# The last two squares of a planned norm: added on VectorE in place of summed as parts on TensorE

## The chip, the cores and the metric

The kernel runs on one core of one Trainium2 chip. The metric is device time in microseconds, the median of several executions. Engines are called by the profile's names: PE (TensorE, matrix products), DVE (VectorE), ACT (ScalarE), POOL (GpSimd), SP (the queue that issues most loads). Each engine runs its instructions in the order in which they were put; they wait for each other by semaphores.

## The reference

A two-layer decoder trunk on one sequence of 512 tokens with a model width of 1024, in float32. Each layer is half a SwiGLU block, a mixer, and half a SwiGLU block; each of the six begins with an RMS norm. Cut to what matters:

```python
def rms_norm(x, g):
    xf = x.astype(jnp.float32)
    y = xf * lax.rsqrt(jnp.mean(xf * xf, axis=-1, keepdims=True) + EPS) * g.astype(jnp.float32)
    return y.astype(x.dtype)

for l in range(DEPTH):
    x = x + 0.5 * swiglu(rms_norm(x, ffn_norm[l, 0]), ...)
    h = rms_norm(x, mix_norm[l])
    x = x + m          # m: hybrid_mixer(h, ...) in layer 0, sparse_attention(h, ...) in layer 1
    x = x + 0.5 * swiglu(rms_norm(x, ffn_norm[l, 1]), ...)
```

What concerns the change is the mean of `xf * xf` over the 1024 features of each token.

## The kernel before

The residual stream lies in SBUF as `xT`, features on partitions: eight blocks `xT[:, j]` of 128 features x 512 tokens. Six stages run one after the other: ffn00, mix0 (the hybrid mixer), ffn01, ffn10, mix1 (attention), ffn11. Every product is made three times from operands split into a high and a low part (`mm3`, L280 to L282): high x high, high x low, low x high. Weights are loaded in blocks (tile `raw`, on SP), split by ACT (L500 or L239) and DVE (L502 or L242) into `form` (or `iw`, `wq` in attention), and multiplied. In some blocks ("summed") the low part is made by a DMA that POOL issues (L529 to L531).

The norm of the next stage is prepared at the end of each stage. The normalising factor of a token is not applied to the input of the next products; they take x times the gain (`xgn`, high and low, L795 on ACT and L798 on DVE), and the factor follows on their results. So the products of the next stage can begin before the factor is known.

`prep_later(which, k, last, ...)` puts this preparation of the blocks k and k+1 into a plan. For each block j: `xgn`, then a square on ACT (L809) into one of four buffers. Block 0's square goes to the buffer `ssq` itself. For the others but the last two, POOL adds the square to `ssq` (`vtt` with `pool=True`, recorded at L495). The last two blocks (j = 4 and 5 behind an FFN, 6 and 7 behind attention) aren't added: their squares are put into the list `ssqs` beside `ssq`, with the first token block for which they count.

`settle_later` then puts, at two fixed places within the first unit of the next stage, the rest: `sums` on PE (L416), one matmul of 128x128 by a column of ones for each of the four token blocks and each part in `ssqs`, into the PSUM tile `pssq`; a scale on DVE (L762); a power on POOL (L764); later transposes on PE into `prow` (L437) and a copy on ACT (L768) into `rrow`, which the evacuation of the first products and the forms of x (L582) read. Behind ffn00, where the mixer's part isn't planned, `settle` and `rms_col` do the same (L428, L429, L464).

What sets the order: `Plan` collects steps with an engine, an estimated duration, reads and writes, computes due times back from PE's stream, and places the steps one by one. PE's steps of one stream stay in the order in which they were added; the steps of the other engines are chosen by when they can start, then by due time. Steps of `vtt` on POOL are estimated at 0.1 us + 2.5 ns per element of a row, on DVE at 0.15 us + 1.05 ns, and the sums at 0.2 us + 0.45 us per part. The mixer of layer 0 is ordered by the scheduler of the language instead. So a changed step can move others of the plan.

Planned norms are four: for mix0, ffn10, mix1 and ffn11. The first norm has no squares of this kind (`load_x`), and the norm for ffn01 is made by `prep`, without a plan; neither is touched. In the norm for ffn11 the squares of blocks 0 to 3 are made and added by halves of 256 tokens.

Of the kernel before, what the change touches and what calls it, by code (L numbers as in the profile page):

```python
# [13 lines left out]
ALU = mybir.AluOpType  # L14
# [4 lines left out]
NB = T // P  # L19
# [194 lines left out]
class Trunk:  # L214
# [557 lines left out]
    def prep_later(self, which, k, last, squares=True, half=None):  # L772

        nc = self.nc
        if k == 0 and not half:
            self.which = which
            self.xgn = [[Lazy(lambda: self.part.tile([P, 4, T], F32R, name="xgn", tag="xg")) for _ in range(2)] for _ in range(2)]  # L780
            squares4 = Lazy(lambda: self.tmp.tile([P, 4, T], F32, name="ssq", tag="ssq", bufs=1))
            self.sqs = [lambda i=i: squares4()[:, i] for i in range(4)]
            self.ssq = self.sqs[0]
            self.ssqs, self.ssqk = [(self.ssq, 0)], ["ssq"]
            self.xg = [LazyFeat(t) for t in self.xgn]
            self.xgk = lambda k: [("xg", which, i, k) for i in range(2)]
        xgn, xT, ssq = self.xgn, self.xT, self.ssq
        halves = (0, 1) if half is None else (half,)
        cols = slice(halves[0] * H, halves[-1] * H + H)
        n = cols.stop - cols.start  # L790
        for j in (k, k + 1):
            g, x = self.gain(which, j), xT[:, j, cols]
            hi, lo = (lambda i=i, j=j: xgn[i][j // 4]()[:, j % 4, cols] for i in range(2))
            hik, lok = ([("xg", which, i, j)] for i in range(2))
            self.s(n, lambda hi=hi, x=x, g=g: nc.scalar.activation(hi(), x, AF.Copy, scale=g), self.xk(j, halves), hik)  # L795

            def low(hi=hi, lo=lo, x=x, g=g, j=j):
                ins = nc.vector.scalar_tensor_tensor(lo(), x, g, hi().bitcast(F32), op0=ALU.mult, op1=ALU.subtract)  # L798
                if j == 0:
                    self.mark = ins  # L800

            self.v(n, low, self.xk(j, halves) + hik, lok)
            if not squares:
                continue
            if j == 0:
                sq, sk = ssq, ["ssq"]
            else:
                sq, sk = self.sqs[1 + j % 3], [("sq", j % 3)]
            self.s(n, lambda x=x, sq=sq: nc.scalar.activation(sq()[:, cols], x, AF.Square), self.xk(j, halves), sk)  # L809
            if last:  # L810
                self.ssqs, self.ssqk = self.ssqs + [(sq, halves[0] * NB // 2)], self.ssqk + sk
            elif j:
                part = [lambda x=x: x()[:, cols] for x in (ssq, sq)]
                self.vtt(n, part[0], *part, ALU.add, ["ssq"], ["ssq"] + sk, True)
        if last:
            self.pending = 1 + squares

# [1076 lines left out]
```

## Time and profile before

| | |
|---|---|
| median of 3 runs | 2018.12 us (2016.62 to 2026.48) |
| profiled execution, its own time | 2019.29 us |
| its span | 2017.6 us |
| mean granted PE clock | 0.992 |
| ACT busy | 1170.2 us |
| instructions | 34412 |

The span is the time from the first to the last recorded instruction. The profile comes as a page (busy times, slices, chain of waits, costliest groups) and as views of the trace. A row of the timeline gives the start, the length in us, the engine, the line of the kernel, the operation, the tile written and the tiles read, shapes and a count; in brackets stands how long the engine was idle before it and what ended that idle time. Rows of the waits and of single tiles give minimum, median and maximum in ns. Rows of the stretches give the length, the busy time of PE, PE's weight loads, DVE, ACT and POOL with counts, the granted PE clock (1.00 is full), the share of the DMA engines, and GB/s. Matmul lengths overlap, so their pace is read from starts.

### The profile page before, as it was taken

What the parts mean: (1) busy time and instruction counts of PE and PEld (TensorE: products, weight loads), DVE (VectorE), ACT (ScalarE), POOL (GpSimd) and SP (SyncE); (2) the same over time, 40 slices, a digit from 0 to 9 for tenths busy, and PEclk for the clock granted to TensorE, in tenths of its full rate; (3) what the DMA queues carried; (4) which work ended last, traced back from release to release, by engine and by line L of the source; (5) the groups of instructions that cost most, each with busy time, mean ns of one, the idle gap of its engine ahead of it and who ended that gap; (6) DMA issues with size and microseconds to landing.
All of it is one profiled execution on the core that took longest, in us unless ns stands there. A gap on an engine that the chain in (4) does not pass through costs nothing.

```text
span 2017.6 us, 34412 instructions
## 1 busy us (share of the span) xinstructions
PE 1984.4 (98%) x13892; PEld 1800.6 (89%) x13892; DVE 1581.4 (78%) x2340; ACT 1170.2 (58%) x1716; POOL 270.1 (13%) x335
## 2 busy tenths in 40 slices
PE   8999999999999999999999999999999999999998
PEld 6999999787788888999998899999965678999998
DVE  6898878886547648988888898978679847988886
ACT  6666657442345434666565575756667644757565
POOL 1000101321101011010002010101215321101010
PEclk9999999999999999999999999999899999999999
DMA  7556566433331232666565356656754202656564
GB/s 210 136 148 167 150 164 148 125 107 115 103 96 63 82 97 63 168 157 162 155 152 149 94 148 167 161 153 160 191 116 105 53 16 69 157 158 165 150 168 115
DMA packets 214439, 265.49 MB, mean 132 GB/s; under 512 B 14140, under 2 KB 187400, under 8 KB 214280
## 3 DMA queue, kind: packets, MB, share of 16 engines
q1 hardware_dynamic: 193632, 190.87, 30.5%
q0 software_dynamic: 20448, 72.36, 19.2%
q8 instruction: 109, 1.79, 0.4%
q14 instruction: 50, 0.41, 0.1%
q10 hardware_dynamic: 200, 0.06, 0.0%
HBM read 188.77 MB, written 2.14 MB: 95 GB/s over the span
## 4 chain that ended last, share of the span: by engine, by line
PE 86%; DVE 5%; DMA 4%; issue 2%; ACT 1%; POOL 1%; SPq 0%; ACTq 0%; POOLq 0%; DVEq 0%
PE pA L281 9%; PE pA L280 9%; PE pA L282 9%; PE pD L280 5%; PE pD L281 5%; PE pD L282 5%; PE pB L280 2%; PE pB L281 2%; PE pB L282 2%; DMA form<-raw 2%; PE po L280 2%; PE po L282 2%; PE po L281 2%; PE ptok L280 2%; PE pu L282 2%
## 5 line engine op out<-in xcount | busy, mean ns | idle before, releaser
L502 DVE TENSOR_TENSOR form<-raw,form 128x1024 fp32r<-128x1024 f32 (+1 forms) x327 | 388.0, 1191 | 113.2 <-ACT form L500 112.3
L500 ACT ACTIVATE form<-raw 128x1024 fp32r<-128x1024 f32 (+1 forms) x327 | 334.6, 1027 | 177.3 <-DVE raw L495 120.6
L280 PE MATMUL pA<-xf,form 128*128 128x256 f32 x1152 | 322.1, 280 | 0.0
L281 PE MATMUL pA<-xf,form 128*128 128x256 f32 x1152 | 321.8, 279 | 0.0
L282 PE MATMUL pA<-xf,form 128*128 128x256 f32 x1152 | 321.4, 279 | 0.0
L495 DVE TENSOR_TENSOR raw<-raw 128x1024 f32<-128x1024 f32 (+2 forms) x241 | 283.6, 1180 | 17.4 <-DMA raw<-in_ffn_w_down 8.6
L530 POOL DMA_DIRECT2D form<-raw x136 | 116.9, 860 | 1202.7 <-ACT form L529 1142.4
L529 ACT ACTIVATE form<-raw 128x1024 fp32r<-128x1024 f32 (+1 forms) x136 | 140.1, 1031 | 140.3 <-PE pD L282 77.4
L280 PEld LDWEIGHTS pA<-xf,form 128*128 128x128 f32 x1152 | 216.4, 188 | 0.2
L282 PEld LDWEIGHTS pA<-xf,form 128*128 128x128 f32 x1152 | 216.1, 188 | 0.0
L281 PEld LDWEIGHTS pA<-xf,form 128*128 128x128 f32 x1152 | 215.8, 187 | 0.2
L281 PE MATMUL pA<-hid,form 128*128 128x256 f32 x704 | 198.6, 282 | 2.8 <-DVE hid L502 2.8
L280 PE MATMUL pA<-hid,form 128*128 128x256 f32 x704 | 198.8, 282 | 0.5 <-ACT hid L500 0.4
L282 PE MATMUL pA<-hid,form 128*128 128x256 f32 x704 | 197.4, 280 | 0.0
L280 PE MATMUL pD<-xf,form 128*128 128x256 f32 x576 | 161.2, 280 | 0.0
L281 PE MATMUL pD<-xf,form 128*128 128x256 f32 x576 | 161.2, 280 | 0.0
L282 PE MATMUL pD<-xf,form 128*128 128x256 f32 x576 | 161.0, 280 | 0.0
L495 DVE TENSOR_TENSOR ft<-ft 128x256 f32<-128x256 f32 (+2 forms) x288 | 146.1, 539 | 4.6 <-ACT ft L748 1.2
L531 ACT ACTIVATE form<-raw 128x1024 fp32r<-128x1024 f32 (+1 forms) x136 | 138.6, 1021 | 0.0
L281 PEld LDWEIGHTS pA<-hid,form 128*128 128x128 f32 x704 | 132.3, 188 | 4.7 <-DVE hid L502 4.6
L280 PEld LDWEIGHTS pA<-hid,form 128*128 128x128 f32 x704 | 132.6, 188 | 1.3 <-ACT hid L500 0.6
L282 PEld LDWEIGHTS pA<-hid,form 128*128 128x128 f32 x704 | 132.3, 188 | 0.0
(447 smaller groups left out, 5191.5 us busy)
## 6 DMA issues: line engine op xcount, KB each, us to landing
form<-raw POOLq DMA_DIRECT2D x120, 512.0 KB, 5.6
raw<-in_ffn_w_gate SPq DMA_DIRECT2D x88, 512.0 KB, 3.8
raw<-in_ffn_w_up SPq DMA_DIRECT2D x88, 512.0 KB, 4.0
raw<-in_ffn_w_down SPq DMA_DIRECT2D x64, 512.0 KB, 4.4
raw<-in_hy_w_in SPq DMA_DIRECT2D x44, 512.0 KB, 3.5
raw<-in_ffn_w_down SPq DMA_DIRECT2D x32, 384.0 KB, 3.4
raw<-in_hy_w_out SPq DMA_DIRECT2D x16, 512.0 KB, 3.3
form<-raw POOLq DMA_DIRECT2D x16, 384.0 KB, 4.2
```

The costliest lines, as they stand in the source:

```text
L280: mm(out, l[0], r[0], start=start, stop=False)
L281: mm(out, l[0], r[1], start=False, stop=False)
L282: mm(out, l[1], r[0], start=False, stop=stop)
L495: (self.p if pool else self.v)(n, lambda: e.tensor_tensor(out(), x(), y(), op=op), reads, writes)
L500: self.s(n, lambda: nc.scalar.activation(hi(), src(), AF.Copy), srck, hik)
L502: n, lambda: nc.vector.tensor_tensor(lo(), src(), hi().bitcast(F32), op=ALU.subtract), srck + hik, lok
L529: self.s(n, lambda: nc.scalar.activation(f()[:, 1], raw, AF.Copy, scale=-1.0), rawk, lok)
L530: self.plan.add("gpsimd", 0.85, lambda: nc.gpsimd.dma_start(f()[:, 1], raw, accum_op=ALU.add), rawk + lok, lok, 5.5)
L531: self.s(n, lambda: nc.scalar.activation(f()[:, 0], raw, AF.Copy), rawk, hik)
```

## The change

The last two squares are no longer kept as parts. Each is added to `ssq` like the others, but on DVE (`pool` is `not last`), so that `ssqs` holds `ssq` alone and `sums` issues one matmul per token block.

```diff
@@ prep_later
             self.s(n, lambda x=x, sq=sq: nc.scalar.activation(sq()[:, cols], x, AF.Square), self.xk(j, halves), sk)
-            if last:
-                self.ssqs, self.ssqk = self.ssqs + [(sq, halves[0] * NB // 2)], self.ssqk + sk
-            elif j:
+            if j:
                 part = [lambda x=x: x()[:, cols] for x in (ssq, sq)]
-                self.vtt(n, part[0], *part, ALU.add, ["ssq"], ["ssq"] + sk, True)
+                self.vtt(n, part[0], *part, ALU.add, ["ssq"], ["ssq"] + sk, not last)
         if last:
             self.pending = 1 + squares
```

With one part, the plan estimates the sums at 0.65 us in place of 1.55.

## The prediction

> **What bounds the kernel now.** I read the page first: busy times, the clock line, the chain of waits.
>
> ```profile
> PE 1984.4 (98%) x13892; PEld 1800.6 (89%) x13892; DVE 1581.4 (78%) x2340; ACT 1170.2 (58%) x1716; POOL 270.1 (13%) x335
> ...
> PEclk9999999999999999999999999999899999999999
> ...
> PE 86%; DVE 5%; DMA 4%; issue 2%; ACT 1%; POOL 1%; SPq 0%; ACTq 0%; POOLq 0%; DVEq 0%
> ```
>
> TensorE is idle for 2017.6 - 1984.4 = 33 us of the span and carries 86% of the chain that ended last. A microsecond of TensorE time saved is a microsecond of the kernel unless TensorE then waits for something else. Next, the view of the tile that receives the sums, and that of the squares.
>
> ```profile
> L416 PE MATMUL pssq<-raw,ssq x120: 164/250/353, 366.5 to 1677.5; 128*128 128x1 f32 x120
> ...
> L809 ACT ACTIVATE ssq<-raw x36: 402/618/634, 348.2 to 1673.5; 128x512 f32<-128x512 f32 x28, 128x256 f32<-128x256 f32 x8
> L495 POOL TENSOR_TENSOR ssq<-ssq x23: 729/1597/2156, 350.1 to 1672.1; 128x512 f32<-128x512 f32 x17, 128x256 f32<-128x256 f32 x6
> ...
> L1055 DVE TENSOR_TENSOR ssq<-ssq,sq x6: 658/688/1007, 618.5 to 668.6; 128x512 f32<-128x512 f32 x6
> ```
>
> A planned norm issues 4 token blocks x 3 parts = 12 matmuls to pssq. There are four planned norms (call them A, before mix0; B, before ffn10; C, before mix1; D, before ffn11) and three others with 4 matmuls: 60 matmuls, recorded as 120, so each fp32 matmul runs as two passes. The last row is the gate's own sum of squares and has exactly the shape of the new VectorE add: 0.69 us.
>
> **What the change does.** Per planned norm it removes 8 of 12 matmuls (16 of 24 passes) and adds two dependent 128x512 adds on VectorE. GpSimd keeps its adds, all that are not the last two. TensorE's sums no longer wait for GpSimd and ScalarE, but for VectorE, which itself waits for both. The instruction order of the built kernel shows the new places; TensorE's sums keep their place among the products in B, C and D (it is the plan's stream) and move by a few in A.
>
> **Norm A.** TensorE's, VectorE's and ScalarE's rows of the timeline:
>
> ```profile
> 369.89 2.29 PE L416 MATMUL pssq<-raw,ssq 128*128 128x1 f32 x20
> 372.03 0.47 PE L281 MATMUL pxbc<-xgn,form 128*128 128x512 f32 x1
> ...
> 363.48 3.77 DVE L798 SCALAR_TENSOR_TENSOR xgn<-raw,xgn 128x512 fp32r<-128x512 f32 x4
> 367.17 1.21 DVE L242 TENSOR_TENSOR form<-raw,form 128x1024 fp32r<-128x1024 f32 x1
> ...
> 369.86 1.06 ACT L239 ACTIVATE form<-raw 128x1024 fp32r<-128x1024 f32 x1 [3.53 <-PE pgate L281]
> ```
>
> Twenty passes fill 372.03 - 369.89 = 2.14 us, 0.107 us each. 16 fewer save 1.71 us. The adds stand right behind the four L798 and end at 367.2 + 2 x 0.69 = 368.6; TensorE reaches the sums at 369.89 less the four passes that ran earlier, 369.5. So there is no wait, with 0.9 us in hand. The weight form behind the adds (L242) goes 1.4 us later; what hides it is that forms run ahead of TensorE (ScalarE's next one stood 3.53 us waiting for a buffer). If that cover were gone, it would cost at most those 1.4 us. **A: -1.7** (-0.3 to -1.7).
>
> **Norm B.** Here VectorE is late already:
>
> ```profile
> 1097.82 0.50 PE L281 MATMUL pg<-xgn,form 128*128 128x512 f32 x1 [0.72 <-DVE xgn L798]
> ...
> 1101.05 3.04 PE L416 MATMUL pssq<-raw,ssq 128*128 128x1 f32 x24
> 1103.95 0.48 PE L280 MATMUL pu<-xgn,form 128*128 128x512 f32 x1
> ...
> 1086.77 2.31 DVE L502 TENSOR_TENSOR form<-raw,form 128x1024 fp32r<-128x1024 f32 x1
> ...
> 1098.29 2.35 DVE L502 TENSOR_TENSOR form<-raw,form 128x1024 fp32r<-128x1024 f32 x2
> 1100.56 2.06 DVE L798 SCALAR_TENSOR_TENSOR xgn<-raw,xgn 128x512 fp32r<-128x512 f32 x3
> ...
> 1084.99 5.24 POOL L495 TENSOR_TENSOR ssq<-ssq 128x512 f32<-128x512 f32 x3 [3.90 <-ACT ssq L809]
> 1094.05 3.17 POOL L495 TENSOR_TENSOR ssq<-ssq 128x512 f32<-128x512 f32 x2 [3.82 <-ACT ssq L809]
> ```
>
> In the new order the adds stand behind the two L502 that end at 1098.29 + 2.35 = 1100.64. Up to there VectorE has the same work in both kernels but one 768-wide form that it now does later (0.87 us), and three of GpSimd's adds come earlier. While GpSimd adds, VectorE's SBUF work is slow: the form at 1086.77 took 2.31 us, A's of that width 1.21. I let these two cancel. Adds end at 1100.64 + 1.38 = 1102.0; eight passes take 0.86; the pu products start at 1102.9 in place of 1103.95. Queued behind the adds are the four L798 of blocks 4 to 7, which TensorE needs only in the second half of the unit, 24 products behind the sums. **B: -1.1**; ends 0 (the form's 0.87 not compensated) and -2.4 (the slow stretch gone earlier, 1.3 us).
>
> **Norm C.** Timeline again:
>
> ```profile
> 1437.58 0.42 PE L281 MATMUL gm<-iw,xgn 128*128 128x64 f32 x1 [3.38 <-DVE iw L502]
> ...
> 1452.40 2.73 PE L416 MATMUL pssq<-raw,ssq 128*128 128x1 f32 x24
> 1455.39 0.40 PE L280 MATMUL gm<-iw,xgn 128*128 128x292 f32 x1 [0.25 <-DVE raw L762]
> ...
> 1425.30 1.06 DVE L502 TENSOR_TENSOR iw<-raw,iw 128x876 fp32r<-128x876 f32 x1
> ...
> 1433.81 2.13 DVE L502 TENSOR_TENSOR iw<-raw,iw 128x876 fp32r<-128x876 f32 x1
> ...
> 1444.78 1.40 DVE L798 SCALAR_TENSOR_TENSOR xgn<-raw,xgn 128x512 fp32r<-128x512 f32 x2
> ```
>
> The adds follow the last L798 (1446.2) and end at 1447.6, 4.8 us before TensorE comes: no wait. The 24 passes took 1455.39 - 0.25 - 1452.40 = 2.74 us, so 16 fewer save 1.8. (An iw form took 1.06 us alone and 2.13 while GpSimd added.) Earlier in C the plan trades places on VectorE: a 768-wide form moves behind two L858 and two iw forms shift. That can stall the last product of the down projection by up to 2.5 us, but TensorE stood 3.38 us at 1437.58 for VectorE anyway, and VectorE's work up to that form is the same; I take 0, ends +1.5 and -0.6. Some loads of sa_w_in change places on SP's queue, and their summing DMAs on GpSimd's; these weights are for the queries, behind the sums, so I take nothing, and 1 us if that cover fails. **C: -1.8**, before the clock.
>
> **Norm D.** TensorE's row, the product behind it, and GpSimd's row:
>
> ```profile
> 1673.78 4.09 PE L416 MATMUL pssq<-raw,ssq 128*128 128x1 f32 x24 [0.87 <-POOL ssq L495]
> ...
> 1677.73 0.77 PE L280 MATMUL pu<-xgn,form 128*128 128x512 f32 x1
> ...
> 1670.24 3.48 POOL L495 TENSOR_TENSOR ssq<-ssq 128x512 f32<-128x512 f32 x2 [4.43 <-ACT ssq L809]
> ```
>
> TensorE now waits for GpSimd until 1673.72. The new chain from there is add 0.69, an L798 that stands between (0.7), add 0.69: 1675.8. Eight passes at this place's pace (4.09 / 24 = 0.17) take 1.4 at most, 0.9 at full clock; I take 1.0, so 1676.8 in place of 1677.73: **D: -0.9**, ends 0 and -1.2. The wait grows by 2.1 us, and what is removed is a little more.
>
> **The clock.** The granted clock by stretches of the timeline (the column before the DMA share):
>
> ```profile
> 372.00:376.00 4.00, 4.00 (x19) 3.31 (x19) 0.33 (x2) 0.00 (x0) 1.04 (x1) 1.00 0.43 131
> ...
> 1104.00:1108.00 4.00, 4.00 (x13) 3.13 (x13) 1.96 (x3) 0.00 (x0) 1.49 (x1) 0.64 0.27 79
> ...
> 1456.00:1460.00 4.00, 3.40 (x18) 3.05 (x17) 2.59 (x8) 1.98 (x6) 0.46 (x1) 0.58 0.97 288
> ...
> 1676.00:1680.00 4.00, 4.00 (x14) 3.52 (x15) 0.31 (x2) 0.00 (x0) 1.02 (x1) 0.50 0.00 0
> ```
>
> Behind the sums of B, C and D the clock falls towards half; behind those of A it does not. So passes of one column, like pauses, seem to count as little work, and a stretch of about 3 us of them brings a slow stretch. In C the sums shrink to 0.9 us without a wait, less than A's 2.1, so I expect no slow stretch: 4.00 x (1 - 0.58) = 1.7 us, of which some was idle; I take **-1.2** (0 to -1.7). In B and D a pause takes the place of the passes, so I take 0, ends -1.7 each and, for B and C's trade together, +1.7.
> The Trainium skill, "TensorE: Matmul & The Clock Gate", Part 1, has the clock halve only after an idle window of about 3.4 us; by that rule alone no pause here would cost clock, the clock term would be 0 and the sum 5.5 us. The rows above differ from it, with 0.50 to 0.64 behind sums that never left TensorE idle that long.
>
> **The sum.** 1.7 + 1.1 + 1.8 + 0.9 + 1.2 = 6.7 us. The profiled execution took 2019.29 us around its span of 2017.6; it lies 1.2 above the median 2018.12 of the runs shown. From the median: 2018.1 - 6.7 = **2011 us**.
>
> **Rivals.**
> *The clock stays up everywhere.* If short sums end the slow stretches of B and D too, 1.7 us each come on top, and B's earlier start 1.3: 2011.4 - 4.7 = 2007. For it: the pattern of A. Against: the pauses in B and D stay.
> *No clock term.* What slows C's clock is not the sums but the pauses around them, and the slow stretch stays: 2018.1 - 5.5 = 2012.6. For it: a 0.25 us pause and a busy ScalarE chain lie behind C's sums. Against: A, C and their clocks. The rule named above would give this too.
> *The gain is refilled.* TensorE arrives earlier and waits for weights or VectorE: about 2017. For it: VectorE is 78% busy and behind in B and C. Against: 33 us of idle time in all, little of it behind the sums.
> *Slower: VectorE's queue decides.* One mechanism: the two adds stand in VectorE's strict order behind forms slowed by GpSimd, so TensorE pauses longer than the passes took, and each long pause costs a slow stretch. In B it loses from the point where the adds end later than 1103.95 - 0.86 = 1103.1, 1.1 us after my estimate. Its price: B +1.5, C's trade +1.5, three more slow stretches of 1.7, less A's 1.7 and C's 1.8: 2018.1 + 4.6 = 2023. For it: 2.31 and 2.13 us for forms that take half. Against: GpSimd's adds are over before VectorE's can start.
> That the change does not do what it says is excluded: the built order has 4 matmuls per norm.
>
> **How the numbers follow.** Forecast 0.38 (2008 to 2014), no clock term 0.12, clock stays up everywhere 0.25, refilled 0.14, slower 0.11. What a measurement can tell from no change is 0.5%, 10.1 us: below 2008.0 lies most of the case in which the clock stays up (0.20) and the forecast's edge (0.08), 0.28; above 2028.2 only the far end of the slower case, 0.05; between, 0.67. The range runs from the clock case less B's and A's ends (2007 - 4) to the refilled case and half of the slower one: 2003 to 2020.
>
> **What would show it.** Right: 8 pssq records per norm at about 0.11 us; a wait of 1 to 3 us for VectorE ahead of them in B and D, none in A and C; a clock near 1.00 behind C's sums; the span shorter step by step at A and C. Wrong: a pause before the sums of B beyond 2 us with a clock of 0.5 behind it, TensorE's wait for the last down product in C above 3 us, or TensorE's idle time growing by as much as its busy time falls.

## The result, and the profile after

The changed kernel's median is 2014.64 us, the kernel before's beside it 2018.40 us, 3.8 us more. The ratio estimated from all these runs is 0.9977, with a 95% interval of 0.9968 to 0.9986, so 4.6 us less (2.8 to 6.5); all ratios below are of this kind (the quotient of the two medians is 0.9981). Run again later (experiment e11 below), it was 0.9974 (0.9964 to 0.9985). This is inside the 0.5% that the prediction called no change, and inside its range; it forecast 6.7 us.

The page of the changed kernel: the span, the busy times, the chain of waits.

```profile
span 2013.1 us, 34292 instructions
...
PE 1972.3 (98%) x13828; PEld 1787.9 (89%) x13828; DVE 1586.4 (79%) x2348; ACT 1170.5 (58%) x1716; POOL 272.4 (14%) x335
...
PE 82%; DVE 6%; DMA 5%; issue 3%; ACT 2%; POOL 1%; SPq 0%; ACTq 0%; DVEq 0%; POOLq 0%
```

Against before, 64 matmul records are gone (13892 - 13828), and VectorE has 8 instructions more. TensorE's busy time fell by 12.1 us, its idle time grew from 33.2 to 40.8 us (2013.1 - 1972.3). So in this pair of profiles 12 us of work left and nearly 8 us of waiting came. The view of the sums' tile, and TensorE's waits with total, number of times and longest in us:

```profile
L416 PE MATMUL pssq<-raw,ssq x56: 164/250/271, 369.7 to 1672.7; 128*128 128x1 f32 x56
```

```profile
PE pssq L416 <- DVE ssq L495: 4.2, 2, 2.6
PE pg L281 <- DVE xgn L797: 4.0, 4, 1.6
...
PE pA L282 <- DVE form L502: 3.3, 1, 3.3
```

120 records became 56: 8 in each planned norm, and 24 in the three others as before. The waits ahead of the sums are new in B and D (the kernel before waited there once, 0.87 us, for GpSimd in D). TensorE's timeline, by norm:

```profile
369.65 0.95 PE L416 MATMUL pssq<-raw,ssq 128*128 128x1 f32 x8
...
1089.61 0.50 PE L281 MATMUL pg<-xgn,form 128*128 128x512 f32 x1 [1.14 <-DVE xgn L797]
1094.19 0.51 PE L281 MATMUL pg<-xgn,form 128*128 128x512 f32 x1 [1.55 <-DVE xgn L797]
1095.46 0.50 PE L281 MATMUL pg<-xgn,form 128*128 128x512 f32 x1 [0.29 <-DVE xgn L797]
1099.22 1.02 PE L416 MATMUL pssq<-raw,ssq 128*128 128x1 f32 x8 [1.65 <-DVE ssq L495]
1100.11 0.74 PE L280 MATMUL pu<-xgn,form 128*128 128x512 f32 x1
...
1432.49 0.58 PE L282 MATMUL pA<-hid,form 128*128 128x256 f32 x1 [3.28 <-DVE form L502]
1450.91 0.94 PE L416 MATMUL pssq<-raw,ssq 128*128 128x1 f32 x8
1452.11 0.40 PE L280 MATMUL gm<-iw,xgn 128*128 128x292 f32 x1 [0.26 <-DVE raw L762]
1455.92 0.33 PE L1463 MATMUL pq<-raw,ri 128*128 128x128 f32 x1 [0.74 <-ACT ri L1475]
...
1671.88 1.05 PE L416 MATMUL pssq<-raw,ssq 128*128 128x1 f32 x8 [2.59 <-DVE ssq L495]
1672.80 0.48 PE L280 MATMUL pu<-xgn,form 128*128 128x512 f32 x1
```

A and C run their sums without a wait, B and D wait for VectorE's second add. In B the three waits for xgn add up to 2.98 us, where the kernel before shows 1.02 and 0.72. In C the last product of the down projection now waits 3.28 us; the 3.38 us that TensorE used to stand for iw (1437.58 in the prediction) are gone.

VectorE's adds, in B and in D:

```profile
1095.33 2.35 DVE L502 TENSOR_TENSOR form<-raw,form 128x1024 fp32r<-128x1024 f32 x2
1097.60 1.48 DVE L495 TENSOR_TENSOR ssq<-ssq 128x512 f32<-128x512 f32 x2
...
1669.89 0.68 DVE L495 TENSOR_TENSOR ssq<-ssq 128x512 f32<-128x512 f32 x1
1670.48 0.74 DVE L797 SCALAR_TENSOR_TENSOR xgn<-raw,xgn 128x512 fp32r<-128x512 f32 x1
1671.15 0.68 DVE L495 TENSOR_TENSOR ssq<-ssq 128x512 f32<-128x512 f32 x1
```

Each add takes 0.7 us, and each stands where the prediction put it in VectorE's order: in B behind two 1024-wide forms, in D with one L798 (now L797) between the two.

The granted clock in stretches of 4 us (the columns as in the prediction):

```profile
1100.00:1104.00 4.00, 4.00 (x13) 3.21 (x13) 2.93 (x5) 0.00 (x0) 1.49 (x1) 0.57 0.29 97
...
1432.00:1436.00 4.00, 3.51 (x16) 3.51 (x17) 4.00 (x6) 1.86 (x6) 0.00 (x0) 0.50 0.35 89
1436.00:1440.00 4.00, 4.00 (x20) 4.00 (x19) 4.00 (x7) 4.00 (x7) 2.35 (x2) 0.50 0.89 272
1440.00:1444.00 4.00, 4.00 (x27) 4.00 (x26) 3.97 (x7) 3.81 (x6) 2.79 (x5) 0.81 1.03 260
...
1456.00:1460.00 4.00, 4.00 (x31) 4.00 (x32) 3.26 (x7) 3.02 (x7) 0.36 (x1) 1.00 0.80 236
...
1676.00:1680.00 4.00, 4.00 (x17) 3.10 (x17) 0.00 (x0) 0.00 (x0) 0.00 (x0) 0.87 0.00 0
```

Behind C's sums the clock is 1.00, where it had been 0.58. Earlier in C it is lower than before. Whether that comes from the change is one of the questions below.

### The profile page after: what moved, and what is told of

Read it like the earlier page. It is cut to its first block, busy times and chain, and to the rows that moved or that the text cites. A ratio compares the mean times of both kernels' runs of the same rounds, so it can differ in the third digit from the quotient of the medians.

```text
span 2013.1 us, 34292 instructions
## 1 busy us (share of the span) xinstructions
PE 1972.3 (98%) x13828; PEld 1787.9 (89%) x13828; DVE 1586.4 (79%) x2348; ACT 1170.5 (58%) x1716; POOL 272.4 (14%) x335
## 4 chain that ended last, share of the span: by engine, by line
PE 82%; DVE 6%; DMA 5%; issue 3%; ACT 2%; POOL 1%; SPq 0%; ACTq 0%; DVEq 0%; POOLq 0%
PE pA L281 9%; PE pA L280 9%; PE pA L282 9%; PE pD L280 4%; PE pD L281 4%; PE pD L282 4%; PE pB L280 2%; PE pB L281 2%; PE pB L282 2%; DMA form<-raw 2%; PE po L280 2%; PE po L282 2%; PE po L281 2%; DMA raw<-in_ffn_w_gate 2%; PE ptok L280 2%
```

## The experiments

The question is how 6.7 us became 4.6: which of the four norms gave what, what the waits cost, and what the clock did. The main theory: the removed passes are worth about what was forecast or more, and the waits for VectorE in B and D give much of it back. The rivals: that the order trade in C is what costs; that waits only move; that the gain comes from something other than the passes.

To compare places, I use the lag: the start of the same product in two traces, at fixed points ahead of and behind each norm (at 355, 385, 1080, 1120, 1415, 1475, 1650 and 1700 us of the first trace of the kernel before; the median over products within 6 us). The change of the lag over a norm is what that norm became longer or shorter. The lost clock is 4 us times (1 - granted clock), summed over the stretches of a norm. In every trace that sum comes out near 0, 1.7, 3.4 or 5.1 us: slow stretches are whole pieces of about 3.4 us at half clock, one or several. A piece made A 1.6 us longer, where TensorE has no waits (e4, e7 in the table below); where TensorE waits anyway, it costs less.

**e1_order_kept.** The two adds are told to the plan as costing nothing, so that VectorE and ScalarE keep the order of the kernel before, with the adds put in.

```diff
-            if j:
+            if j and last:
+                self.plan.add("vector", -0.25 * (j % 2 == 0), lambda sq=sq: nc.vector.tensor_tensor(
+                    ssq()[:, cols], ssq()[:, cols], sq()[:, cols], op=ALU.add), ["ssq"] + sk, ["ssq"])
+            elif j:
```

> The changed kernel, but the plan is told that the two new adds take no time, so that in the down products ahead of B, C and D every instruction of VectorE and ScalarE keeps the order of the kernel before and only the two adds are put in. Theory 1 (what C lost, it lost through the plan's new order): TensorE's wait of 3.28 us for a form in C's last down product is gone, the wait of 3.4 us for an iw form is back, C gains about 3 us against the kernel before in place of 1.2, and the whole is 7 to 9 us faster than before (2010). Theory 2 (the adds and the waits for them cost it, whatever the order): about 2014, like the change.

Ratio 0.9976 (0.9965 to 0.9987), the same as the change. TensorE's waits:

```profile
PE pssq L416 <- DVE ssq L811: 5.7, 2, 2.9
...
PE gm L281 <- DVE iw L502: 3.4, 1, 3.4
```

The 3.28 us wait in C is gone and the 3.4 us for iw is back in its place. In B, too, a wait only moves: TensorE waits 1.75 us for xgn, as in the kernel before, in place of 2.98, so it comes 1.2 us earlier to the sums and waits 2.92 us there in place of 1.65. So the trade moves waits of the same size and does not change the total by an amount that these times can tell.

**e2_thrice.** The adds stay, but each sum is issued three times over the one part, and the factor is divided by three: the passes of before, with the order and the waits of after.

```diff
-            self.t(0.2 + 0.45 * len(ssqs), lambda: self.sums(ps(), [(x(), b) for x, b in ssqs]), self.ssqk, ["pssq"])
-            self.v(4, lambda: nc.vector.tensor_scalar(ms, ps()[:, 0:NB], 1.0 / D, EPS, op0=ALU.mult, op1=ALU.add),
+            self.t(0.65, lambda: self.sums(ps(), [(x(), b) for x, b in ssqs]), self.ssqk, ["pssq"])
+            self.v(4, lambda: nc.vector.tensor_scalar(ms, ps()[:, 0:NB], 1.0 / (D * len(ssqs)), EPS, op0=ALU.mult, op1=ALU.add),
...
+            self.ssqs = 3 * self.ssqs
```

> The changed kernel, with each matmul of the sums issued three times over the one summed part and the scale divided by three: VectorE's adds stay, and the 24 passes per norm are back. Theory 1 (the gain is the 16 passes and the clock behind them): A's sums 1.7 us longer, C's 1.7 and a slow stretch of the clock behind them again (about 1.5), B's and D's 1.7 each and slow stretches; together 8 to 12 us slower than the change, 2023 to 2026. Theory 2 (the passes are cheap, the gain is that the sums no longer wait for GpSimd or ScalarE): under 4 us slower than the change.

Ratio 1.0025 (1.0009 to 1.0040): 5 us slower than before, so the change without its saving of passes costs 5 us (1.8 to 8.1), and the 64 passes are worth 1.0025 - 0.9977 of 2018 us, 9.7 us, known to some 3.6 us either way. By their own length, 64 x 0.107, they are 6.9. The passes are what gains, and the adds and waits are what loses; a gain from the new order alone is excluded.

```profile
PE 1981.3 (98%) x13892; PEld 1796.2 (89%) x13892; DVE 1586.1 (79%) x2348; ACT 1170.6 (58%) x1716; POOL 271.5 (13%) x335
```

```profile
368.00:372.00 4.00, 4.00 (x30) 3.65 (x29) 1.39 (x2) 1.06 (x1) 0.86 (x1) 0.87 0.52 155
372.00:376.00 4.00, 4.00 (x14) 3.21 (x13) 0.00 (x0) 0.00 (x0) 0.18 (x1) 0.71 0.33 111
```

The first row is the page's, with the matmul count of before; the others are clock stretches at A. Here A's 24 passes brought a slow stretch, which they had not in the profile before; behind C's sums, where one was expected, this trace has none.

**e3_late_BD.** Sums and row of B and D are settled later, at places (2, 4) of the stream in place of (1, 3).

```diff
-                if 2 * qs[0] + i in ((2, 4) if late else (1, 3)):
+                if 2 * qs[0] + i in ((2, 4) if late or self.which in (2, 3) else (1, 3)):
```

> The changed kernel, with the sums of B and D and their rows half a weight block (24 products, 5.5 us) later in TensorE's stream. Theory 1 (the waits of 1.65 us in B and 2.59 us in D before the sums are on the path): no wait before the sums, no slow stretch of the clock behind D's, 4 to 7 us faster than the change, 2008 to 2011. Theory 2 (TensorE only waits elsewhere, for the forms of x that need the row, 5.5 us later): within 1.5 us of the change, with new waits for xf or for pg's buffers in the units behind.

Ratio 0.9976 (0.9964 to 0.9988). Two rows of TensorE's timeline say why it isn't better:

```profile
1100.51 1.02 PE L416 MATMUL pssq<-raw,ssq 128*128 128x1 f32 x8
1151.47 0.39 PE L282 MATMUL pA<-xf,form 128*128 128x256 f32 x1 [1.68 <-DVE form L502]
...
1670.77 1.87 PE L416 MATMUL pssq<-raw,ssq 128*128 128x1 f32 x8 [2.82 <-DVE ssq L495]
```

B's sums no longer wait, but 50 us later TensorE waits 1.68 us for a form, and the same way 1.48 us in D's unit at 1724.85; the changed kernel has neither wait. This fits the row, and with it the forms of x on VectorE, coming later. D's sums wait as before, as if the plan had pulled other products ahead: against the changed kernel, counted from D's start, the sums come 3.0 us later and VectorE's adds 3.5.

**e4_only_C** and **e7_only_B.** The change in one norm alone (`which` is 5 for C, 2 for B; the other norms keep their parts).

```diff
-            if j:
+            if last and which != 5:
+                self.ssqs, self.ssqk = self.ssqs + [(sq, halves[0] * NB // 2)], self.ssqk + sk
+            elif j:
```

> The change in C alone; A, B and D keep three parts. Theory 1 (the pieces of the trace add up): 1 to 1.5 us faster than before, with a 3 us wait for a form in the last down product and no slow stretch behind C's sums. Theory 2 (what C shows depends on what A and B did before it, through the phase of the clock's stretches): another number, 0 or 3 us.

> The change in norm B alone. Theory (B gains nothing in its place: passes saved are paid by a wait of 1.65 us and longer waits for xgn): ratio 1.000, within 1 us of before; PE's wait for ssq of 1 to 2 us at B and none elsewhere new. By the prediction's term: 1.1 us faster, 0.9995. The two are too near for the times; the profile's wait and offset decide.

C alone: 0.9985 (0.9968 to 1.0001), which holds both the 1 to 1.5 us of the theory and nothing. B alone: 1.0001 (0.9988 to 1.0014), with the waits of the changed kernel:

```profile
1097.74 0.50 PE L281 MATMUL pg<-xgn,form 128*128 128x512 f32 x1 [1.53 <-DVE xgn L798]
1099.00 0.50 PE L281 MATMUL pg<-xgn,form 128*128 128x512 f32 x1 [0.29 <-DVE xgn L798]
1102.76 1.02 PE L416 MATMUL pssq<-raw,ssq 128*128 128x1 f32 x8 [1.64 <-DVE ssq L495]
```

So B gives nothing by itself that the times can tell, and the waits are those of the change in B, whatever the other norms do.

**e5_sums_late** and **e6_before_sums_late.** Only the sums of B and D move, to place 2; the row stays at place 3. In e6 the same is done to the kernel before.

```diff
-                if 2 * qs[0] + i in ((2, 4) if late else (1, 3)):
+                if 2 * qs[0] + i in ((2, 4) if late else (2, 3) if self.which in (2, 3) else (1, 3)):
```

> The change, with the sums of B and D put one place of the stream further back (behind the third group of products instead of the second), while the row of factors keeps its place, so that nothing that reads the row comes later. Theory (in B the wait for VectorE's adds, 1.65 us, and the slow stretch behind it eat what the removed passes save): no wait ahead of B's sums, clock near 1.00 behind them, B's offset against before 2 to 3 us better than the change's 0, no new wait at the forms of x behind the row; D's wait of 2.6 us stays, because the plan pulls other products ahead and the sums still come right when x is ready. Total 2 to 3 us below the change, about 2012, ratio 0.9965. Rival (the wait only moves: xgn of the second half of the blocks is late whatever the sums do): the wait turns up at the next products that need VectorE, total as the change, 0.9977.

> The kernel before with only that move of the sums, 12 matmuls as before: the control for the run above. If the move alone brings what the run above gains over the change, it is the place and not the pair of place and fewer passes: 0.9985 to 1.000 here. The theory says nearly nothing (before waits 0.9 us for GpSimd in D and not at all in B): within 1 us of before, 1.000.

e5: 0.9977 (0.9962 to 0.9992). e6: 0.9981 (0.9968 to 0.9993). The middle of e5 is the rival's, and its interval just holds the 0.9965 of the theory: the times don't decide. e6 misses. In e5's trace B's wait is gone, as the row shows, and its slow stretches too: B is 4.62 us shorter than in the first trace of before (the changed kernel's is 0.34 shorter); yet the middle ratio is the change's. And the move alone, without the change, gained 3.9 us, where nothing was expected.

```profile
1104.64 1.02 PE L416 MATMUL pssq<-raw,ssq 128*128 128x1 f32 x8
```

That the measured gains don't follow the profiles norm by norm has a plain limit: e5's ratio is known to 1.5 parts in a thousand and the change's to 0.9, so a difference of 2 or 3 us could hide between them. In e6 the plan places VectorE's work otherwise, too: two waits for xgn of 1.02 and 0.72 us are replaced by 0.85 and 0.28 ahead of the sums. That is 0.6 us of the 3.9.

**e8_order_kept_sums_late.** e1 and the move of e5 together, the candidate for the best.

> The kernel of e1_order_kept with the sums of B and D one place further back: the candidate for the best of all. In e1 the sums of B and D waited 2.9 us each for VectorE. Theory: B's wait goes, 2 to 3 us below e1, about 0.9963. Rival (waits only move): as e1, 0.9976.

0.9990 (0.9977 to 1.0003): a miss. TensorE waits 4.89 us ahead of B's sums (TensorE's and VectorE's rows):

```profile
1107.42 1.84 PE L416 MATMUL pssq<-raw,ssq 128*128 128x1 f32 x8 [4.89 <-DVE ssq L811]
...
1102.12 3.75 DVE L798 SCALAR_TENSOR_TENSOR xgn<-raw,xgn 128x512 fp32r<-128x512 f32 x4
1105.79 1.48 DVE L811 TENSOR_TENSOR ssq<-ssq 128x512 f32<-128x512 f32 x2
```

With the adds planned as free, the plan puts them behind four L798 (3.75 us), so that TensorE reaches even the moved sums before the adds are done.

**e9_A_and_C, e10_A_and_C_sums_late, e11_change_again.** The change in A and C only (`last and which not in (4, 5)` keeps the parts in the other two); the same with the sums of B and D moved as in e6; and the changed kernel itself again.

> The change in A and C alone, B and D as before. Theory (only where the adds end before TensorE comes is anything gained; in B and D the adds are paid for by the waits ahead of the sums): A -1.8 and C -1.8 and what the clock gives in C, so 3.5 to 5 us faster than before, ratio 0.998, the same as the whole change within its interval. Rival (the gain is spread over all four norms, as the prediction had it, 2.0 of 6.7 in B and D): 2 us slower than the whole change, 0.9987.

> A and C changed, and in B and D the move of the sums of e6_before_sums_late, which alone gave 0.9981. Theory (the gains lie in different norms and add up): 0.998 x 0.9981, about 0.996, 8 us faster than before and 3 us faster than the change. Rival (single ratios here are mostly the clock's chance, and what one place wins another gives back): 0.9978, no better than either.

> The changed kernel once more, beside the two above on the same chip, and a second profile of the same program: how far the offsets of the norms and the slow stretches of the clock differ between two executions of one program. Ratio 0.9977 as at first; the waits ahead of the sums of B and D the same to 0.1 us; the number of slow stretches per norm not the same.

e9: 0.9985 (0.9969 to 1.0001). e10: 0.9981 (0.9968 to 0.9993). e11: 0.9974 (0.9964 to 0.9985). A and C alone give some 3 us (0 to 6), and the whole change beside them, on the same chip, 5. These intervals overlap, so it isn't settled, but the middle values are nearer to the rival (0.9987, B and D give their share) than to my theory that B and D give nothing. The gains of e6 and e9 do not add up in e10. No version beat the change.

e11 is a second profile of one program, and shows what differs by chance:

```profile
1098.38 0.51 PE L281 MATMUL pg<-xgn,form 128*128 128x512 f32 x1 [1.55 <-DVE xgn L797]
1099.64 0.50 PE L281 MATMUL pg<-xgn,form 128*128 128x512 f32 x1 [0.29 <-DVE xgn L797]
...
1103.41 1.08 PE L416 MATMUL pssq<-raw,ssq 128*128 128x1 f32 x8 [0.34 <-DVE ssq L495]
```

The waits for xgn are the same to 0.01 us. The wait ahead of B's sums is 0.34 us in place of 1.65, against what I expected: the slow stretch lay ahead of the sums in this execution, so TensorE came later and VectorE was nearly done. The stretch that holds them:

```profile
1100.00:1104.00 4.00, 3.66 (x13) 2.49 (x12) 3.90 (x6) 1.40 (x3) 0.00 (x0) 0.57 0.48 150
```

A wait and a slow stretch cover each other. Early in C this execution lost 1.7 us of clock, the first one 5.1.

**e12_before_again.** The kernel before, a second profile.

> The kernel before once more, for a second profile of the same program, as e11_change_again is for the change. The ratio must be 1.000 within its interval. Theory (24 passes in one go bring a slow stretch of 3.4 us or not, by chance; 8 do not): behind the sums of A or C at least one slow stretch; ahead of D's sums the wait of 0.87 us as in the first profile. Rival (the slow stretches behind C's sums in the first profile came from something else): none behind A's or C's sums in two more looks of this kind would speak for it.

Ratio 1.0008 (0.9995 to 1.0021). The profiled execution:

```profile
span 2013.0 us, 34412 instructions
...
PE 1979.9 (98%) x13892; PEld 1796.6 (89%) x13892; DVE 1581.9 (79%) x2340; ACT 1170.2 (58%) x1716; POOL 269.4 (13%) x335
```

```profile
1456.00:1460.00 4.00, 4.00 (x32) 3.88 (x30) 2.35 (x5) 3.79 (x8) 0.91 (x1) 1.00 1.07 378
...
1676.00:1680.00 4.00, 4.00 (x14) 3.21 (x13) 0.00 (x0) 0.00 (x0) 0.00 (x0) 0.72 0.00 0
```

The same program, 4.6 us shorter in its span than in the first profile (2017.6), as much as the whole effect of the change. Against what I expected, there is no slow stretch behind the sums of A or C this time; the wait of 0.88 us in D is there. Of the 12.1 us by which TensorE's busy time fell in the first pair of profiles, 4.5 (1984.4 - 1979.9) lie between these two executions of the kernel before. One pair of profiles can't give the size of an effect like this one; only what repeats in all of them, and the medians, can.

## Why the prediction was right, and where not

The lags of all the traces, with the lost clock of each norm in brackets, in us, one execution each. Each figure is the change of that norm's length against the first trace of the kernel before:

| trace | A | B | C | D |
|---|---|---|---|---|
| before | 0 [0] | 0 [3.4] | 0 [5.1] | 0 [3.4] |
| before, e12 | 0.00 [0] | -1.55 [1.7] | -1.78 [1.7] | -0.01 [3.4] |
| after | -1.68 [0] | -0.34 [1.7] | -1.37 [5.1] | -1.78 [1.7] |
| after, e11 | -1.68 [0] | -1.86 [1.7] | -3.16 [1.7] | -1.81 [1.7] |
| e1 | -1.67 [0] | -0.22 [1.7] | -2.27 [1.7] | -1.53 [1.7] |
| e7, only B changed | 1.60 [1.7] | -0.33 [1.7] | 0.62 [5.1] | -0.05 [3.4] |
| e4, only C changed | 1.59 [1.7] | 1.63 [5.1] | -0.82 [5.1] | -1.66 [1.7] |
| e9, A and C changed | -1.67 [0] | -1.58 [1.7] | -3.66 [1.7] | -1.67 [1.7] |
| e2, changed, 24 passes | 1.69 [1.7] | 1.51 [3.4] | -2.18 [1.7] | 0.03 [1.7] |
| e3, changed, B and D later | -1.68 [0] | -4.64 [0] | -3.23 [1.7] | -0.04 [3.4] |
| e5, changed, B's and D's sums later | -1.68 [0] | -4.62 [0] | -3.11 [1.7] | -1.45 [1.7] |
| e6, before, B's and D's sums later | 0.01 [0] | -2.38 [1.7] | -0.32 [3.4] | -1.66 [1.7] |
| e8, e1 and e5 together | -1.68 [0] | 0.06 [3.4] | -2.37 [3.4] | 0.06 [3.4] |
| e10, A and C changed, B's and D's sums later | -1.68 [0] | -0.75 [3.4] | -0.79 [5.1] | -1.59 [1.7] |

To compare places within a norm, a time can be put on the time of the first trace of the kernel before, by taking off the lag that the trace had ahead of the norm (for the changed kernel -3.53 us in B and -3.55 in D). Times given "on the first trace's time" are of this kind.

*A, forecast -1.7.* Right to a few hundredths at equal clock: -1.67 or -1.68 in all eight traces with 8 passes in A. What it missed is the clock: "Behind the sums of B, C and D the clock falls towards half; behind those of A it does not" holds for one execution. With 24 passes in A, three of six traces show a slow stretch at the sums (e2, e4, e7), which makes A about 1.6 us longer; with 8 passes, none of eight.

*B, forecast -1.1.* Here the forecast was too good, in two steps of it. The first is "I let these two cancel", which says when VectorE is done. The adds take what was said and stand where it was said, but on the first trace's time the two forms ahead of them end at 1095.33 + 2.35 + 3.53 = 1101.2, not at 1100.64, and the adds at 1102.6, not at 1102.0. (In e11 and e7 it is 1102.6, too.) So the first pu product starts at 1103.6, where the forecast had 1102.9.

The second step is what the forecast was measured against. In the one execution that it was read from, a slow stretch lay ahead of B's sums (granted clock 0.78 from 1096 to 1100), so TensorE reached them only at 1101.05. e12 and e9 have none there; e12's rows:

```profile
1097.77 2.74 PE L416 MATMUL pssq<-raw,ssq 128*128 128x1 f32 x24
1100.37 0.48 PE L280 MATMUL pu<-xgn,form 128*128 128x512 f32 x1
```

On the first trace's time (lag -2.02) these start at 1099.8 and 1102.4. Without that slow stretch the kernel before is through all 24 passes before VectorE of the changed kernel has even ended its adds. The change then costs 1103.6 - 1102.4 = 1.2 us, and the waits add up to that: for xgn 1.24 us more (2.98 - 1.74), 1.65 ahead of the sums, less 1.71 for 16 passes (2.60 against 0.89). In e1 the waits for xgn are those of before and the wait ahead of the sums is longer instead, with the same result: what decides is the end of the adds, not where TensorE waits for it.

The table agrees. At the same lost clock of 1.7 us, unchanged B is at -1.55 and -1.58, changed B at -0.22 to -0.34 in three traces. e11's -1.86 is no exception: its slow stretch lay ahead of the sums, where TensorE would have waited for VectorE otherwise, and the others' lay behind the sums. So B by itself costs about 1.2 us. Against that stands one slow stretch less, 1.7 us in the four traces with the change in its place against 3.4, 1.7, 5.1 and 1.7 without; so few traces can't tell that from chance. The means over the table (unchanged: before, e12, e4, e9; changed: after, e11, e1, e7) are -0.38 and -0.69: a gain of 0.3, and e7's time agrees (1.0001).

*C, forecast -1.8 and -1.2 for the clock.* At equal lost clock C gives -1.37 (after against before, 5.1 both) and -1.38 (e11 against e12, 1.7 both), in place of -1.8. The passes saved just that: 2.74 us between the first pass and what follows became 1452.11 - 0.26 - 1450.91 = 0.94. The two pairs lose the other 0.4 in two ways. In after and before, TensorE's waits in C add up to the same (4.27 and 4.24 us; the one for ri behind the sums is 0.14 longer, the one early in C 0.10 shorter), but of this waiting only about 1.2 us lies in slow stretches, against 2.0 before, so 0.4 us more of lost clock is paid. In e11 against e12 the waits grow by 0.4 us, from 4.6 to 5.0. TensorE now comes early enough to stand for ScalarE ahead of attention's first lg products:

```profile
1460.64 0.70 PE L1590 MATMUL lg<-keys,ri 64*128 64x256 f32 x4 [0.71 <-ACT ri L1469]
```

The same wait is 0.49 us in e9, 0.68 in e3, 0.96 in e5 and 1.45 in e1, all with 1.7 us of lost clock; no trace with 24 passes in C has it. The trade, "I take 0", is no loss by itself: at that lost clock C is at -2.27 in e1, without the trade, and at -3.11 to -3.66 in the four traces with it. But "TensorE's wait for the last down product in C above 3 us" came true, which the prediction had listed among the things that would show it wrong. The clock behind C's sums is 1.00 in all nine traces in which C has 8 passes; with 24, two of five show a slow stretch (1.7 us in before, 3.4 in e7). On the mean, 5.1 / 5 = 1.0 us an execution, near the -1.2. The low clock earlier in C, 3.4 us in the first trace of before and 5.1 in that of after, is chance: e11 has 1.7 with the same program.

*D, forecast -0.9.* The means of the traces are -0.68 unchanged (before, e12, e7, e4, e9) and -1.71 changed (after, e11, e1): 1.0. The chain of adds ended at 1671.15 + 0.68 = 1671.83, on the first trace's time 1675.4, and its order was as written; the forecast had 1675.8. TensorE's wait grew by 1.7 us (2.59 - 0.87), forecast 2.1. But the 4.09 us of passes that the forecast took away belong to one execution, in which a slow stretch began among them. From the first pass to the next product it is 3.95 us there and 2.70 in e9 and e4, where it begins later; e9's rows:

```profile
1666.05 2.84 PE L416 MATMUL pssq<-raw,ssq 128*128 128x1 f32 x24 [0.87 <-POOL ssq L495]
1668.75 0.61 PE L280 MATMUL pu<-xgn,form 128*128 128x512 f32 x1
```

On the first trace's time that next product starts at 1676.48 in e9 (lag -7.73) and at 1676.35 in the changed kernel. And at an equal lost clock of 1.7 us unchanged D is at -1.66 and -1.67, changed D at -1.53 to -1.81. So without the clock D gives about 0.1. The rest of the 1.0 is one slow stretch less: three of the five unchanged traces lost 3.4 us in D, none of the three changed ones did. The prediction put the clock's share in D at 0, though "this place's pace" had part of it in; and eight traces can't tell this share from chance. The size of D is right for another reason, and in part by luck.

*The sum.* The means of the norms give A 2.3 (-1.67 against a mean of 0.64 over before, e12, e4, e7 and e6's 0.01), B 0.3, C 1.9 (-2.26 against -0.37 from before, e12, e7 and e6's -0.32; changed: after, e11, e1, e4, e9) and D 1.0: 5.5 us, and the times 4.6 and 5.2. So 6.7 was 1.5 to 2 us too much, and it lies in B (0.8) and C (1.1); A gave 0.6 more than forecast. What was mis-sized is, in B, the wait for VectorE, whose adds ended 0.6 us later than forecast, and in C what TensorE pays behind the passes saved (0.4); the clock behind C's sums was 0.2 short, and the last 0.5 of C are the slow stretches early in C, 3.1 us on the mean of these changed traces against 2.6, which is chance. The clock's share in A and D, put at 0, made up for part of it. One bound of the range does not come out of its terms: the 4 us below 2007 are called the ends of B and A, but A's forecast was its end already and B's 1.3 us are in the 2007. Nothing hung on it.

*The rivals.* "The gain is refilled" holds in part, in B and D, and by the wait for ri in C: by e2 the adds and their order take 5 us of the 9.7 that the passes give. "The clock stays up everywhere" holds behind the sums of A and C, and not in B and D, where a pause stands ahead of them. "VectorE's queue decides" has its mechanism right in B and D, but the pauses brought no more slow stretches than there were; e8, with its 4.89 us, shows what comes when the adds end too late.
The Trainium skill, "TensorE: Matmul & The Clock Gate", Part 1, describes the clock's window as free-running, 3413 ns long and not tied to the kernel, with other results from run to run. The traces agree with that: pieces of 3.4 us, and the same program with 1.7 or 5.1 us lost in C. Its rule that the clock halves after an idle window of that length doesn't fit: at the sums of A, 24 passes brought half clock in three of six traces, with TensorE busy for 4.00 of 4.00 us (e2's rows).

## What stays open

Why the move of the sums alone gains 3.9 us (e6; 1.4 to 6.5), while it adds nothing that the times can tell to the change (e5) or to its half (e10): by the lags, e6's B is 0.8 us shorter than e12's at the same lost clock, and e5's B has no wait left but those of before. Whether B and D together bring the 2 us between e9 and e11: the intervals overlap. And whether the change itself makes slow stretches rarer in B and D, as the few traces suggest.

## What to carry to other kernels

A run of one-column products can cost more than its own length when it is long enough to bring a slow stretch of the clock, so ask of such a run what the clock does behind it, in more than one execution. An add moved to another engine costs nothing where it ends well ahead of the reader (A and C) and is paid for by a wait where the reader stands right behind the last input (B and D): look at that distance first. And profile each program twice before reading a difference of a few us out of two traces, or a forecast out of one: here a slow stretch of that one execution was priced into B and D as if it were the kernel's.

## What the hardware showed that I had not expected

The clock differs between executions of one program by as much as the change was worth: two of the kernel before lost 11.9 and 6.8 us to slow stretches in the four norms together, and of the changed kernel 8.5 and 5.1. Eight passes (0.95 us) never brought one in A or C, in 17 cases; 24 passes (2.3 us for the last 20 in A, 2.73 us in C) did in 5 of 11. If the two were alike, all five would fall to the longer runs with a chance of 462/98280, 0.5%, taking the cases as independent.
